# Pinning the sixth form's weight sums of the second MLP's first two pairs in VectorE's program order

## The chip, the cores and the metric

The kernel runs on one core of a Trainium2 chip. Time is device microseconds of one execution, and the median of several executions is what is compared. A profiled execution is slower or faster by a few microseconds than the timed ones, so its own time is given beside it.

## The reference

A two-layer encoder trunk on x of 1024 positions by 1024 features, in float32. Layer 0 mixes tokens by grouped-query attention, layer 1 by a chunked gMLP; each layer ends in a dense squared-ReLU MLP, and every sub-layer is normalized, modulated and added back with a gate:

```
mod = cond @ ada_w[i] + ada_b[i];  sh1, sc1, g1, sh2, sc2, g2 = split(mod, 6)
h = modulate(rmsnorm(x, norm1_g[i]), sh1, sc1)
y = gqa_attention(h, ...) if i % 2 == 0 else chunked_gmlp(h, ...)
x = x + g1 * y
h = modulate(rmsnorm(x, norm2_g[i]), sh2, sc2)
x = x + g2 * (square(relu(h @ w_in[i])) @ w_out[i])      # 1024 -> 4096 -> 1024
```

The change lies in the first product of the second MLP (h @ w_in[1]).

## The kernel before

Everything is kept transposed: features on the 128 partitions, positions along the free axis, in two halves of 512 positions. Every float32 product is made from three faster products: an operand is split into a rounded part "hi" (a cast on ScalarE, L333 for activations, L459 for weights) and a rest "lo" (a subtraction on VectorE, L334 and L460), and TensorE adds hi·hi, hi·lo and lo·hi. The large products further use Winograd's seven-product form of a 2 by 2 block product. Here the blocks of a weight are its quarters: two adjacent 128-column slices of the weight (a "pair") times the two halves of the 1024 inputs. Quarter 11, 12 belong to the pair's first slice (one 512 KB tile `raws[2p]`), 21, 22 to its second (`raws[2p+1]`).

`winograd` runs the first product of each MLP. A unit (q, p) is form q of pair p: twelve 128x512 matmuls (L474 to L476) into one PSUM bank. The second MLP has 16 pairs. With FIRST = 6, forms 1 and 2 of pairs 0 to 5 come first (units 0 to 11), since their activations are ready first; then each pair's forms 6, 5, 4, 7, 3 (pair 0 is units 12 to 16, pair 1 units 17 to 21); pairs 6 and up run all seven forms in a row. The weights of pairs 0 and 1 are loaded whole at the start and stay; those of pairs 2 to 5 pass once for forms 1 and 2 (L427, into t tiles) and are loaded again for the rest. There are four 512 KB buffers of tag w, so pair 2's weights are loaded when pair 0's last readers are done (L421, in `prep` of form 3).

`prep` makes a unit's weights, LA = 3 units ahead of its matmuls in the order of the code. For form 6 it adds quarter 22 to quarter 21 in place (L452) and subtracts quarter 11 from that into quarter 11 (L453). Forms 5, 4, 7 and 3 of the pair all go on from there: form 5 reads the sum in 21; L456 (prepared with form 4) subtracts the new 11 from 12 for form 3; L458 (form 7) subtracts the new 11 from 22. Only form 4's own operand, quarter 22 as loaded, needs none of it. The result goes into one of five s buffers as hi and lo. L482, L485, L488, L490, L493, L496 and L500 are VectorE's readings of the finished products.

What runs between: `mlp` calls a hook after each unit. In the second MLP (HB = 2, 1 and HR = 2, 1, so the second of each) step 1 starts the second half's norm (L280, L282, L287, the power on GpSimd at L242, L294), step 2 calls `forms_b`, steps 3 to 6 make the activations of form 6 (L339, L381, L382, L393 and a split), and steps 7, 8, 9 and 10 split those of forms 5, 4, 7 and 3, four splits each.

The code gives no final order. The framework orders each engine's instructions itself from a model of the machine: an instruction is issued when the model has its inputs ready, an earlier one in the code first where several are ready. Work whose inputs are ready early so floats far ahead of its place in the code. `pin` (L51) takes that freedom away: it puts an instruction behind the one traced just before it on its engine, with no wait. On the chip each engine works its queue in that fixed order and each instruction waits for its own inputs.

The second MLP's first loads and preps are traced two units before the end of the gMLP's output product (`if i == out_.n - PRE: next(mlp1)`); the class `Out` runs that product (matmuls L1215 to L1217, weight casts L1197 and L1198, activations loaded from DRAM by L1173 and split by L333 and L334, PSUM read by L1234 and L1267, weight sums on GpSimd by L1183 and following).

## Time and profile before

| | |
|---|---|
| median of 3 timed executions | 2616.09 us (2610.80 to 2616.37) |
| the profiled execution's own time | 2620.57 us |
| its span, first to last instruction | 2618.8 us |
| TensorE busy | 2593.0 us, 99% of the span |
| VectorE busy | 2179.8 us, 83% |
| ScalarE busy | 1443.7 us, 55% |
| GpSimd busy | 718.5 us, 27% |
| mean granted TensorE clock | 0.998 |
| L452, all 44 instructions | 32.5 us |
| VectorE idle before L452 until a load of the MLPs' first weight landed | 2.4 us, 3 times |

The span lies 1.8 us inside the execution's time; what is outside does not change with an order on VectorE. Busy time of TensorE counts matmuls from start to modelled end and they overlap, so 99% says that it hardly ever stands still, and the idle time before a matmul says where it does. Names such as L452 are lines of the kernel as printed above.

### The profile page before, as it was taken

What the parts mean: (1) busy time and instruction counts of PE and PEld (TensorE: products, weight loads), DVE (VectorE), ACT (ScalarE), POOL (GpSimd) and SP (SyncE); (2) the same over time, 40 slices, a digit from 0 to 9 for tenths busy, and PEclk for the clock granted to TensorE, in tenths of its full rate; (3) what the DMA queues carried; (4) which work ended last, traced back from release to release, by engine and by line L of the source; (5) the groups of instructions that cost most, each with busy time, mean ns of one, the idle gap of its engine ahead of it and who ended that gap; (6) DMA issues with size and microseconds to landing.
All of it is one profiled execution on the core that took longest, in us unless ns stands there. A gap on an engine that the chain in (4) does not pass through costs nothing.

```text
span 2618.8 us, 37177 instructions
## 1 busy us (share of the span) xinstructions
PE 2593.0 (99%) x12808; PEld 2167.8 (83%) x12808; DVE 2179.8 (83%) x3281; ACT 1443.7 (55%) x2584; POOL 718.5 (27%) x527
## 2 busy tenths in 40 slices
PE   9999999999999999999999999999999999999999
PEld 7889999887788888888888888888788788888887
DVE  7878999887989999877987687778889977789974
ACT  4579999845644555345543454445456644455442
POOL 0237876433000005430122055442420000005400
PEclk9999999999999999999999999999999999999999
DMA  8100222233586798544243454568641554497461
GB/s 289 45 1 9 89 82 76 89 130 128 195 284 242 279 310 301 181 137 169 81 153 113 137 175 169 174 216 298 228 142 52 182 176 159 148 313 264 150 212 58
DMA packets 209327, 434.33 MB, mean 166 GB/s; under 512 B 23089, under 2 KB 35505, under 8 KB 209138
## 3 DMA queue, kind: packets, MB, share of 16 engines
q1 hardware_dynamic: 182258, 394.19, 44.7%
q10 hardware_dynamic: 26880, 37.76, 4.0%
q8 instruction: 101, 1.65, 0.3%
q14 instruction: 88, 0.72, 0.1%
HBM read 309.18 MB, written 122.68 MB: 165 GB/s over the span
## 4 chain that ended last, share of the span: by engine, by line
PE 83%; DVE 9%; DMA 3%; ACT 3%; issue 1%; POOL 1%; SPq 0%; DVEq 0%; ACTq 0%; POOLq 0%
PE w L474 10%; PE w L475 10%; PE w L476 10%; PE out L1215 9%; PE out L1216 9%; PE out L1217 9%; PE s L952 4%; PE o L988 4%; PE t L969 4%; PE v L1574 3%; PE v L1573 3%; PE v L1572 3%; PE mix L1679 1%; DVE t L334 1%; DMA t<-hf 1%
## 5 line engine op out<-in xcount | busy, mean ns | idle before, releaser
L1215 PE MATMUL out<-t,s 128*128 128x512 f32 x1232 | 480.1, 390 | 2.5 <-ACT t L333 2.5
L1216 PE MATMUL out<-t,s 128*128 128x512 f32 x1232 | 480.0, 390 | 1.6 <-DVE t L334 1.6
L1217 PE MATMUL out<-t,s 128*128 128x512 f32 x1232 | 479.4, 390 | 0.0
L474 PE MATMUL w<-t,s 128*128 128x512 f32 x1168 | 458.5, 394 | 1.8 <-DVE c L1683 1.2
L475 PE MATMUL w<-t,s 128*128 128x512 f32 x1168 | 455.2, 390 | 1.8 <-DVE t L334 1.8
L476 PE MATMUL w<-t,s 128*128 128x512 f32 x1168 | 454.7, 389 | 0.0
L334 DVE TENSOR_TENSOR t<-t,t 128x512 fp32r<-128x512 f32 x408 | 323.8, 804 | 27.4 <-ACT t L333 20.2
L333 ACT CAST t<-t 128x512 fp32r<-128x512 f32 x408 | 244.8, 617 | 121.1 <-DMA t<-hf 71.3
L1215 PEld LDWEIGHTS out<-t,s 128*128 128x128 f32 x1232 | 231.6, 188 | 51.6 <-ACT t L333 3.7
L1216 PEld LDWEIGHTS out<-t,s 128*128 128x128 f32 x1232 | 231.7, 188 | 50.4 <-DVE t L334 2.9
L1217 PEld LDWEIGHTS out<-t,s 128*128 128x128 f32 x1232 | 231.7, 188 | 48.4
L459 ACT CAST s<-w 128x512 fp32r<-128x512 f32 x292 | 173.5, 616 | 161.8 <-PE w L476 104.7
L474 PEld LDWEIGHTS w<-t,s 128*128 128x128 f32 x1168 | 219.4, 188 | 49.6 <-issue 3.5
L475 PEld LDWEIGHTS w<-t,s 128*128 128x128 f32 x1168 | 219.4, 188 | 48.7 <-DVE t L334 5.2
L460 DVE TENSOR_TENSOR s<-w,s 128x512 fp32r<-128x512 f32 x292 | 221.8, 766 | 43.7 <-ACT s L459 43.0
L1197 ACT CAST s<-t 128x512 fp32r<-128x512 f32 x240 | 148.4, 621 | 197.2 <-PE out L1217 143.8
L476 PEld LDWEIGHTS w<-t,s 128*128 128x128 f32 x1168 | 219.3, 188 | 45.3
L1198 DVE TENSOR_TENSOR s<-t,s 128x512 fp32r<-128x512 f32 x240 | 195.7, 816 | 63.9 <-ACT s L1197 63.1
L1183 POOL TENSOR_TENSOR w<-w,t 128x512 f32<-128x512 f32 x20 | 33.5, 1684 | 765.7 <-DVE t L334 345.8
L955 DVE TENSOR_REDUCE mx<-s 128x1 f32<-128x1024 f32 x128 | 156.2, 1221 | 27.2 <-PE s L952 25.5
L978 DVE TENSOR_TENSOR t<-t,t 128x512 fp32r<-128x512 f32 x256 | 164.2, 682 | 17.3 <-ACT t L972 16.2
L988 PE MATMUL o<-t,t 128*128 128x256 f32 x1024 | 163.5, 292 | 0.0
(259 smaller groups left out, 5060.7 us busy)
## 6 DMA issues: line engine op xcount, KB each, us to landing
t<-hf SPq DMA_DIRECT2D x320, 256.0 KB, 4.0
hf<-c SPq DMA_DIRECT2D x156, 256.0 KB, 3.1
w<-in_wi_dram SPq DMA_DIRECT2D x64, 512.0 KB, 4.3
hf<-c ACTq DMA_DIRECT2D x96, 256.0 KB, 2.3
w<-in_ada_dram SPq DMA_DIRECT2D x36, 512.0 KB, 4.1
x<-in_ada_dram SPq DMA_DIRECT2D x64, 256.0 KB, 5.9
t<-in_wm_dram SPq DMA_DIRECT2D x64, 256.0 KB, 4.9
wf<-w SPq DMA_DIRECT2D x64, 256.0 KB, 2.9
```

The lines of the kernel that those rows point to most:

```text
L333: S.copy(hi, src)
L334: (eng or V).tensor_tensor(lo, src, f32(hi), ALU.subtract)
L459: S.copy(hi, src)
L460: V.tensor_tensor(lo, src, f32(hi), ALU.subtract)
L474: T.matmul(ps, hi[:, a], th, start=kt == 0, stop=False)
L475: T.matmul(ps, hi[:, a], tl, start=False, stop=False)
L476: T.matmul(ps, lo[:, a], th, start=False, stop=kt == 3)
L988: pin(T.matmul(u.po, vt[st][:, u.g * P : (u.g + 1) * P], src[:, s * 256 : (s + 1) * 256], start=st == 0 and part == 0, stop=st == 7 and pa ...
L1198: V.tensor_tensor(lo, src, f32(hi), ALU.subtract)
L1215: T.matmul(ps, hi[:, a], th, start=begin and kt == 0, stop=False, **g)
L1216: T.matmul(ps, hi[:, a], tl, start=False, stop=False, **g)
L1217: T.matmul(ps, lo[:, a], th, start=False, stop=end and kt == 3, **g)
```

## The change

`winograd` gets a flag that only the second MLP sets (layer == 1). With it, the addition of quarter 22 into quarter 21 for form 6 is pinned for pairs 0 and 1. Computation, tiles, loads and engines stay as they are; the framework makes its order anew from the added constraint.

```
-    def winograd(wsrc, npair, f, sink, first=0, hook=None, begin=None):
+    def winograd(wsrc, npair, f, sink, first=0, hook=None, begin=None, stay_=False):
...
                 a11, a21, a22 = (half(p, c) for c in ("11", "21", "22"))
-                V.tensor_tensor(a21, a21, a22, ALU.add)
+                ins = V.tensor_tensor(a21, a21, a22, ALU.add)
+                if stay_ and p < 2:
+                    pin(ins)
                 V.tensor_tensor(a11, a21, a11, ALU.subtract)
...
-        yield from winograd(lambda m: t["wi"][layer, m], 16, f, sink, FIRST, at, lambda: (cut(8), f.update(fs[0])))
+        yield from winograd(lambda m: t["wi"][layer, m], 16, f, sink, FIRST, at, lambda: (cut(8), f.update(fs[0])),
+                            layer == 1)
```

## The prediction, on record before the result

> **What bounds the kernel now.** I read the page first: is any engine but TensorE a bound?

> ```profile
> span 2618.8 us, 37177 instructions
> PE 2593.0 (99%) x12808; PEld 2167.8 (83%) x12808; DVE 2179.8 (83%) x3281; ACT 1443.7 (55%) x2584; POOL 718.5 (27%) x527
> ```

> TensorE stands still for at most 2618.8 - 2593.0 = 25.8 us of the whole kernel, so no order on VectorE can win more, and one that starves TensorE costs in full: nothing behind it is idle enough to give time back. VectorE's 83% is a mean; what counts is whether it is behind at the places that the four moved instructions leave or enter. So next comes the chain of waits around 1857 us, where L452 (the sum) of the second MLP's pairs 0 and 1 runs today, within the gMLP's output product:

> ```profile
> 1850.43 7.25 DMA w<-in_wi_dram
> ...
> 1862.60 0.46 DVE w L452
> ...
> 1867.63 1.77 DVE t L334
> 1869.43 0.63 ACT t L333
> 1870.14 0.76 PE out L1215
> ```

> The chain that sets the end runs from a load of the MLP's weight through L452 into an activation split and then a matmul. VectorE's timeline of the same place shows why:

> ```profile
> 1855.45 0.68 DVE L1198 TENSOR_TENSOR s<-t,s 128x512 fp32r<-128x512 f32 x1
> 1857.70 0.69 DVE L452 TENSOR_TENSOR w<-w 128x512 f32<-128x512 f32 x1 [1.57 <-DMA w<-in_wi_dram]
> 1858.31 0.68 DVE L334 TENSOR_TENSOR t<-t,t 128x512 fp32r<-128x512 f32 x1
> ...
> 1862.52 1.78 DVE L452 TENSOR_TENSOR w<-w 128x512 f32<-128x512 f32 x1
> 1864.22 0.68 DVE L1267 TENSOR_TENSOR t<-out,t 128x512 f32<-128x512 f32 x1
> 1864.83 1.19 DVE L334 TENSOR_TENSOR t<-t,t 128x512 fp32r<-128x512 f32 x1
> 1865.93 1.78 DVE L1198 TENSOR_TENSOR s<-t,s 128x512 fp32r<-128x512 f32 x1
> 1867.63 1.76 DVE L334 TENSOR_TENSOR t<-t,t 128x512 fp32r<-128x512 f32 x1
> ```

> The first sum holds the queue 1.57 us for its load and 1858.31 - 1857.70 = 0.61 us for itself; the second takes 1864.22 - 1862.52 = 1.70 us. Together 3.88 us, and from the first to the split at 1867.63 the queue never rests, so they are queued straight into that split. TensorE's timeline, and the stretches with the granted clock (busy time of PE, PEld, DVE, ACT and POOL with its instructions; then the clock, the DMA share and GB/s):

> ```profile
> 1859.16 0.39 PE L1217 MATMUL out<-t,s 128*128 128x512 f32 x1
> 1859.74 0.47 PE L1215 MATMUL out<-t,s 128*128 128x512 f32 x1 [0.19 <-ACT t L333]
> ...
> 1867.78 0.39 PE L1217 MATMUL out<-t,s 128*128 128x512 f32 x1
> 1870.14 0.76 PE L1215 MATMUL out<-t,s 128*128 128x512 f32 x1 [1.97 <-ACT t L333]
> ...
> 1873.64 0.39 PE L1217 MATMUL out<-t,s 128*128 128x512 f32 x1
> ```

> ```profile
> 1852.00:1868.00 16.00, 15.81 (x70) 12.60 (x68) 14.43 (x20) 8.44 (x15) 5.59 (x4) 1.00 0.99 372
> 1870.00:1872.00 2.00, 1.86 (x5) 1.50 (x6) 2.00 (x4) 0.21 (x2) 0.00 (x0) 0.54 0.00 0
> 2095.00:2270.00 175.00, 175.00 (x773) 144.96 (x773) 133.28 (x209) 85.26 (x144) 0.00 (x0) 1.00 0.47 162
> ```

> The last row gives the pitch of a matmul, 175.00 / 773 = 0.226 us. So the small stop costs 1859.74 - 1859.16 - 0.23 = 0.35 us, the large one 1870.14 - 1867.78 - 0.23 = 2.13 us. Behind the large one the granted clock is 0.54, and the nine matmuls from 1870.14 to 1873.64 take 3.50 us instead of 9 x 0.226 = 2.03: another 1.47 us. All in all 3.95 us hang on this place.

> [...]

> **The change, part by part.** Pinning adds no instruction, wait or DMA: it moves. Each pinned sum takes with it all that goes on from it, and the rows show how far that work runs ahead today:

> ```profile
> 1992.61 0.69 DVE L453 TENSOR_TENSOR w<-w,w 128x512 f32<-128x512 f32 x1
> ...
> 1997.80 0.69 DVE L456 TENSOR_TENSOR w<-w 128x512 f32<-128x512 f32 x1
> ...
> 2002.86 0.68 DVE L460 TENSOR_TENSOR s<-w,s 128x512 fp32r<-128x512 f32 x1
> ...
> 2006.32 0.68 DVE L460 TENSOR_TENSOR s<-w,s 128x512 fp32r<-128x512 f32 x1
> ...
> 2009.16 0.69 DVE L458 TENSOR_TENSOR w<-w,w 128x512 f32<-128x512 f32 x1
> ```

> By the order of the code these are pair 0's L453 and L456, the rests of its forms 6 and 5, and its L458; pair 1's L453 and L456 lie between them.

> *Removed at 1857 (gain).* Which of the 3.88 us reach TensorE? Not all: GpSimd's four adds run right behind, and each VectorE operation with two inputs in SBUF is stretched beside them (1.19 to 1.78 above against 0.68), sum or no sum.

> ```profile
> 1862.41 6.43 POOL L1183 TENSOR_TENSOR c<-c,t 128x512 f32<-128x512 f32 x4 [11.03 <-DMA t<-in_wgo_dram]
> ```

> Without the sums L1267 can start when its unit's product is there, about 1859.74 + 12 x 0.226 + 0.39 = 1862.8 instead of 1864.22; the three stretched operations follow, and the split ends near 1867.9 instead of 1867.63 + 1.76 = 1869.39, 1.5 us earlier. The stop of 2.13 shrinks to about 0.6, the small one goes, the clock stays up; but with TensorE earlier, the later splits can be late by some tenths. 0.35 + 1.5 + 1.47 is 3.3; I take 3.0. Bounds: 3.95 (all of it), and 0.4 if the loads, which use 0.99 of the DMA time here, keep the splits late and only the small stop goes. What is late next in either case is L333 waiting for `t<-hf`.

> *Where the sums go.* Pair 0 is prepared in step 12 - 3 = 9. The last VectorE instruction traced before it is the last split of form 4's activations, in step 8. Pair 1 (unit 17, step 14) comes behind L488 of pair 0's form 5. In today's queue the first place is the last row here:

> ```profile
> 2034.12 0.68 DVE L485 TENSOR_TENSOR c<-w,c 128x512 f32<-128x512 f32 x1
> ...
> 2042.32 0.68 DVE L482 TENSOR_TENSOR c<-w,c 128x512 f32<-128x512 f32 x1
> 2042.92 0.68 DVE L334 TENSOR_TENSOR t<-t,t 128x512 fp32r<-128x512 f32 x1
> ```

> L485 reads pair 0's finished form 6, so unit 12 is computed before 2034 today, and its weights cannot exist before 2042.92 + 0.68 = 2043.6 in that queue after the change. What does TensorE lose? The stretches of the stage, all engines, and (last row) the matmuls with weights from s buffers alone:

> ```profile
> 2011.40:2024.90 13.50, 13.50 (x61) 11.13 (x60) 13.34 (x22) 10.06 (x16) 0.00 (x0) 1.00 0.00 1
> 2024.90:2041.30 16.40, 14.83 (x64) 11.67 (x63) 16.20 (x28) 13.33 (x25) 0.00 (x0) 1.00 0.38 128
> 2041.30:2053.70 12.40, 12.40 (x56) 10.26 (x55) 11.98 (x20) 9.30 (x18) 0.00 (x0) 1.00 0.26 86
> ```

> ```profile
> 2027.65:2041.30 13.65, 4.06 (x15) 1.00 0.45 154
> ```

> From 2027.65 the second forms of pairs 3 to 5 run, whose weights are split late, and 15 matmuls of pair 0 (twelve of form 6, three of form 5) fill the pauses: 15 x 0.226 = 3.4 us that have no such filler after the change. VectorE is full (13.34 of 13.50, 16.20 of 16.40, 11.98 of 12.40): the sums arrive where it has no room. In its favour, the rests of pair 0's forms 7 and 3 and of pair 1's form 6, L485, and pair 2's L452 and L453, which stand ahead of 2042.92 today, move behind too: six operations of 2042.92 - 2042.32 = 0.60 us. Of these 3.6 us ScalarE's casts (13.33 of 16.40 busy) allow perhaps 2.4. So the split ends near 2041.2, L452 near 2041.8, the cast of form 5's weights near 2042.5. The chain of waits tells when the second forms end:

> ```profile
> 2033.74 0.62 ACT s L459
> ...
> 2036.98 0.52 ACT t L333
> 2037.54 0.50 PE w L474
> ```

> The last of them starts at 2037.54 for a cast, and on its path lies a floated cast for pair 1's form 6 (0.62), which the pin sends away: start near 2037.0, end 12 x 0.226 = 2.7 us later, near 2039.7. From there TensorE can run pair 0's form 4, whose weights need no sum and whose activations come from just those splits, until about 2042.5, and find form 5 ready. At 2045.1 it has then done 48 + 12 + 12 = 72 matmuls since 2024.9; today 64 until 2041.3 (its row) and 17 more, 80 without the one that both ends cut. Eight fewer are 1.8 us. Seven sums and two rests, 9 x 0.60 = 5.4 us of work, come into a queue that is full until 2053.7, so a few tenths more are lost. I take 2.0 in all. Bounds: 9.5 us (rival 2), and -1.0 if the floated cast leaves the path and nothing starves.

> *Queues past which work moves.* On SP, pair 2's two loads wait for pair 0's last readers, the rests of forms 7 and 3:

> ```profile
> 2029.46 7.14 SPq L421 DMA_DIRECT2D w<-in_wi_dram  x2
> ```

> They come some 15 to 20 us later, and are needed ten units (27 us) behind form 6 of pair 0: covered. Without that cover each microsecond late would be one lost. Pair 1's pin waits for TensorE to finish form 5; behind it VectorE holds L490 and the next rests, three units ahead of their use. GpSimd issues nothing there.

> *Sum.* -3.0 + 2.0 = -1.0 us on the profiled execution's 2620.57, 2619.6; the median of the runs, 4.5 below that execution, becomes 2615.1. I say 2615.

> **The rivals.**

> 1. *The stop at 1870 goes and nothing starves.* For it: the filling between 2027 and 2041 shows that the framework takes whatever is ready. -3.95 - 1.0 = -5 us: 2611. Against: 15 fillers are gone for certain, and VectorE has no room.

> 2. *The start of the MLP starves (the other side).* If form 4's weights are not prepared ahead and VectorE's queue doesn't move up, L452 begins at 2043.6 and form 5's cast ends 0.6 + 0.6 + 0.1 later, at 2044.9. The second forms end at 2037.54 + 2.7 = 2040.3: TensorE stands 4.6 us, with the lost filling of 3.4 that is 8.0, and a stop longer than 1.97 us brings the slow clock again, 1.5: 9.5 us, less 3.0 is +6.5, 2622.6. With VectorE 2.4 us ahead it is +4: 2620. It decides from 5 us of loss at the start.

> 3. *The stop at 1870 stays, since the loads are what is late.* ScalarE's casts there do wait for `t<-hf`; against it, the very cast before the stop waits for VectorE (the chain's L334). -0.4 + 2.0: 2617.7. If the slow clock doesn't follow from the stop, the gain is 3.0 - 1.5 and the result 2616.6, in the same case. [...]

> 4. *The pin changes nothing*, if the model's order already had the sums there. The rows at 1857 refute it; 2616.

> **How the numbers follow.** Forecast 0.42 (2612.5 to 2617.5), rival 1 0.21, rival 2 0.17, rival 3 with the slow-clock case 0.17, rival 4 0.03. About 5 us (0.2%) is what a measurement of this kernel can tell from no change; the three runs alone spread by 5.6. Faster by more: most of rival 1 and a little of the forecast, 0.19. Slower by more: two thirds of rival 2 and some of 3, 0.14. Within: 0.67. The range 2608.5 to 2622 takes in rival 1's 2611 with the runs' spread, and all but the dear end of rival 2.

> **What would show it.** Right: L452 has no load to wait for and none lies between 1850 and 1990; no stop over 1 us near 1868 and a granted clock of 1.00 there; L452 of pair 0 directly behind a split near 2041; matmuls of form 4 before L485. Wrong: a stop at 1868 that still ends on L334 or on `t<-hf`; a stop of 2 us or more between 2030 and 2046, with a granted clock near 0.5 behind it; stops between 2050 and 2070, which would mean that the 5.4 us of moved work were not absorbed.

## The result, and the profile after

The changed kernel takes 2625.17 us in the median of 6 executions (2618.26 to 2628.46), the kernel before 2615.10 us beside it (2610.80 to 2616.37): a ratio of 1.0042, interval 1.0026 to 1.0057. Timed again later with more executions (below) it is 1.0026, interval 1.0015 to 1.0036. So the change makes the kernel slower by some 7 to 11 us, where 1 us faster was forecast; both medians (the second is 2622.95) lie above the forecast range, which ends at 2622.

The profiled execution took 2618.26 us and was the quickest of its six. Its page:

```profile
span 2616.5 us, 37187 instructions
PE 2588.2 (99%) x12808; PEld 2163.6 (83%) x12808; DVE 2179.6 (83%) x3281; ACT 1447.2 (55%) x2584; POOL 716.1 (27%) x527
...
L476 PE MATMUL w<-t,s 128*128 128x512 f32 x1168 | 459.4, 394 | 5.0 <-ACT s L461 4.4
```

The totals tell nothing: TensorE and VectorE are as busy as before, and this span is even shorter than before's. The one new thing is the end of the last line: 4.4 us in which TensorE waited for L461, the cast of a weight (L459 before; the new lines move every number behind them by two or three: the matmuls are L476 to L478, the rest of a weight L462, the subtraction L455, VectorE's reading of the second form L484).

What moved is seen when each product is taken from its first matmul to the next product's first. The stretches of the gMLP's output product and of the second MLP's first product, in the kernel before (columns: length, then busy time and count of PE, PEld, DVE, ACT and POOL, then granted clock, DMA share, GB/s):

```profile
1766.91:2001.65 234.74, 231.86 (x1017) 190.95 (x1016) 205.26 (x289) 119.83 (x209) 62.21 (x41) 0.99 0.58 200
2001.65:2309.93 308.28, 306.40 (x1354) 252.87 (x1352) 248.68 (x395) 168.47 (x286) 1.43 (x1) 1.00 0.47 161
```

and in the changed kernel:

```profile
1760.93:1991.38 230.45, 229.74 (x1017) 189.95 (x1016) 202.69 (x281) 119.70 (x209) 61.96 (x41) 1.00 0.59 200
1991.38:2307.54 316.16, 308.92 (x1353) 253.49 (x1352) 251.45 (x399) 167.81 (x285) 1.01 (x1) 0.99 0.46 157
```

The first gains 234.74 - 230.45 = 4.29 us, the second loses 316.16 - 308.28 = 7.88 us. The stretches that the change doesn't touch differ by a few us from one execution to the next (in the twelve profiles of this study the part ahead of the first MLP takes 630 to 637 us, and the gMLP's part just ahead of its output product 279 to 284 us), which is why a single span misleads here.

The place that the prediction looked at first, VectorE and TensorE about 1868 us, is quiet. The stretches there, in the changed kernel:

```profile
1852.00:1868.00 16.00, 16.00 (x72) 13.24 (x72) 14.93 (x20) 8.20 (x14) 7.37 (x5) 1.00 0.78 282
1868.00:1872.00 4.00, 4.00 (x20) 3.30 (x19) 4.00 (x5) 0.62 (x1) 2.59 (x2) 1.00 0.41 131
```

No stop, and a granted clock of 1.00. The loss lies in the second MLP. TensorE's timeline there:

```profile
2021.70 0.50 PE L478 MATMUL w<-t,t 128*128 128x512 f32 x1 [1.10 <-DVE t L334]
...
2025.54 0.50 PE L476 MATMUL w<-t,t 128*128 128x512 f32 x1 [1.24 <-ACT t L333]
...
2028.59 0.39 PE L478 MATMUL w<-t,t 128*128 128x512 f32 x1
2033.42 0.50 PE L476 MATMUL w<-t,s 128*128 128x512 f32 x1 [4.44 <-ACT s L461]
```

The last second form ends (2028.59), and the next matmul, form 6 of pair 0, starts 4.83 us later. Behind it the clock falls:

```profile
2028.59:2033.42 4.83, 0.39 (x2) 0.00 (x0) 4.40 (x8) 2.87 (x7) 0.00 (x0) 1.00 0.26 98
2033.42:2037.30 3.88, 3.56 (x8) 2.45 (x9) 3.88 (x7) 3.59 (x7) 0.00 (x0) 0.56 0.00 0
```

At the pitch of 0.226 us, the stop costs 4.83 - 0.23 = 4.60, the eight matmuls behind it 3.88 - 1.81 = 2.07 (0.32 of them a second wait, for the rest of the weight), the two smaller stops 1.26 and 1.40 (1.10 and 1.24 of idleness, and 0.16 each by which a matmul's modelled duration of 0.39 is longer than the pitch). Together 9.3; before had one stop here, 1.57 us of idleness, 1.73 in all. 9.3 - 1.7 = 7.6 of the 7.88; the rest are stops of tenths.

Why form 6 comes so late is on VectorE's timeline and, in the last row, ScalarE's:

```profile
2029.02 0.69 DVE L484 TENSOR_TENSOR c<-w,c 128x512 f32<-128x512 f32 x1 [1.25 <-PE w L478]
2029.63 1.28 DVE L334 TENSOR_TENSOR t<-t,t 128x512 fp32r<-128x512 f32 x2
2030.83 0.68 DVE L452 TENSOR_TENSOR w<-w 128x512 f32<-128x512 f32 x1
2031.43 0.68 DVE L334 TENSOR_TENSOR t<-t,t 128x512 fp32r<-128x512 f32 x1
2032.03 0.68 DVE L455 TENSOR_TENSOR w<-w,w 128x512 f32<-128x512 f32 x1
```

```profile
2032.75 0.62 ACT L461 CAST s<-w 128x512 fp32r<-128x512 f32 x1 [0.83 <-DVE w L455]
```

At the head of VectorE's queue stands L484, the reading of the very second form that TensorE is just computing: it waits 1.25 us for it, and the sum stands three operations behind. So form 6 cannot begin before the second form has ended and six operations of VectorE and a cast have followed. And nothing else is there for TensorE. The casts of weights into s buffers, in the changed kernel between 1975 and 2037 us and in the one before between 1985 and 2046 (duration min/median/max in ns, then first and last start):

```profile
L461 ACT CAST s<-w x7: 603/618/626, 1981.0 to 2034.8; 128x512 fp32r<-128x512 f32 x7
```

```profile
L459 ACT CAST s<-w x11: 605/622/627, 1991.2 to 2045.6; 128x512 fp32r<-128x512 f32 x11
```

The seven are four ahead of the MLP (1981 to 1989, forms 1 and 2 of pairs 0 and 1) and three from 2032.75 on (forms 6, 5 and 4 of pair 0, by the order of the code). Before, form 6, 5 and 4 of pair 0 followed the first four at 2001.85, 2005.58 and 2007.78. Form 4, which needs no sum, came behind form 6 all the same.

### The profile page after: what moved, and what is told of

It is laid out like the page before. It is cut to its first block, busy times and chain, and to the rows that moved or that the text cites. A ratio compares the mean times of both kernels' runs of the same rounds, so it can differ in the third digit from the quotient of the medians.

```text
span 2616.5 us, 37187 instructions
## 1 busy us (share of the span) xinstructions
PE 2588.2 (99%) x12808; PEld 2163.6 (83%) x12808; DVE 2179.6 (83%) x3281; ACT 1447.2 (55%) x2584; POOL 716.1 (27%) x527
## 4 chain that ended last, share of the span: by engine, by line
PE 87%; DVE 7%; ACT 2%; DMA 2%; issue 1%; SPq 0%; POOL 0%; DVEq 0%; ACTq 0%
PE out L1218 11%; PE out L1217 11%; PE out L1219 11%; PE w L476 10%; PE w L478 10%; PE w L477 10%; PE s L954 4%; PE o L990 4%; PE t L971 4%; PE v L1577 3%; PE v L1576 3%; PE v L1575 3%; PE mix L1682 2%; DVE t L334 1%; PE wo L926 1%
## 5 line engine op out<-in xcount | busy, mean ns | idle before, releaser
L1217 PE MATMUL out<-t,s 128*128 128x512 f32 x1232 | 479.2, 389 | 1.1 <-ACT t L333 1.1
L476 PE MATMUL w<-t,s 128*128 128x512 f32 x1168 | 459.4, 394 | 5.0 <-ACT s L461 4.4
L478 PE MATMUL w<-t,s 128*128 128x512 f32 x1168 | 455.3, 390 | 0.3 <-DVE s L462 0.3
L334 DVE TENSOR_TENSOR t<-t,t 128x512 fp32r<-128x512 f32 x408 | 326.2, 810 | 26.2 <-ACT t L333 18.9
L333 ACT CAST t<-t 128x512 fp32r<-128x512 f32 x408 | 245.0, 617 | 114.0 <-DMA t<-hf 63.3
L461 ACT CAST s<-w 128x512 fp32r<-128x512 f32 x292 | 174.4, 617 | 182.6 <-PE w L478 125.4
L1217 PEld LDWEIGHTS out<-t,s 128*128 128x128 f32 x1232 | 231.2, 188 | 49.6 <-ACT t L333 1.5
L1218 PEld LDWEIGHTS out<-t,s 128*128 128x128 f32 x1232 | 231.3, 188 | 49.5 <-DVE t L334 1.9
L1219 PEld LDWEIGHTS out<-t,s 128*128 128x128 f32 x1232 | 231.3, 188 | 48.0
L476 PEld LDWEIGHTS w<-t,s 128*128 128x128 f32 x1168 | 219.7, 188 | 52.7 <-ACT s L461 5.0
L478 PEld LDWEIGHTS w<-t,s 128*128 128x128 f32 x1168 | 219.6, 188 | 46.2 <-DVE s L462 0.9
L462 DVE TENSOR_TENSOR s<-w,s 128x512 fp32r<-128x512 f32 x292 | 220.1, 760 | 41.6 <-ACT s L461 41.1
```

The costliest lines, as they stand in the source:

```text
L333: S.copy(hi, src)
L334: (eng or V).tensor_tensor(lo, src, f32(hi), ALU.subtract)
L461: S.copy(hi, src)
L462: V.tensor_tensor(lo, src, f32(hi), ALU.subtract)
L476: T.matmul(ps, hi[:, a], th, start=kt == 0, stop=False)
L478: T.matmul(ps, lo[:, a], th, start=False, stop=kt == 3)
```

## The experiments

For each kernel the ratio to the kernel before on the same chip, and the two stretches read from its profile as above (before: 234.7 and 308.3 us):

| kernel | ratio, interval | gMLP output product | second MLP's first product |
|---|---|---|---|
| before, again | one execution | 231.8 | 308.3 |
| the change | 1.0042, 1.0026 to 1.0057 | 230.5 | 316.2 |
| the change, again | 1.0026, 1.0015 to 1.0036 | 231.3 | 316.3 |
| sums free, subtraction pinned | 1.0032, 1.0021 to 1.0044 | 233.4 | 316.1 |
| only pair 0 pinned | 1.0025, 1.0014 to 1.0036 | 232.6 | 316.4 |
| only pair 1 pinned | 0.9989, 0.9980 to 0.9997 | 230.5 | 308.3 |
| change, form 4 ahead | 1.0013, 1.0004 to 1.0021 | 230.5 | 313.9 |
| both pinned, step 7 | 1.0011, 1.0001 to 1.0020 | 230.7 | 312.6 |
| both pinned, step 4 | 1.0009, 0.9999 to 1.0020 | 230.8 | 313.2 |
| both pinned, start of the MLP | 1.0002, 0.9993 to 1.0011 | 230.5 | 309.5 |
| both pinned, behind the second unit's weights | 0.9985, 0.9976 to 0.9993 | 230.5 | 308.2 |

**The kernel before, once more.** No edit; it asks how much of the gain is the execution's.

> The kernel before once more, unchanged, for a second profile of it. In the first profile the gMLP's output product lasted 234.75 us and held the stop of 2.13 us with the slow clock at 1868, the second MLP's first product 308.27 us. Theory A (the change wins 4 us at 1868 and loses 8 us at the start of the second MLP): the stop is there again, 233 to 235 us, and 308 us behind it. Theory C (the stop at 1868 was that one execution's, so that the change has nothing to win there): no stop over 1 us at 1868 and about 230.5 us, as after the change.

Measured: the MLP's product is the same to 0.01 us, the gMLP's output product 2.95 us shorter than in the first profile. The stop near 1868 was only 0.76 us of idleness here, without a slow clock, and 231.8 lies between the two theories' figures. So 2.95 of the 4.29 us that the first profile offered to gain there are not there every time.

**The sums free, the subtraction pinned.** Both sums are traced at step 6 without a pin, so that they run in the gMLP as before; L453's subtraction is pinned in their place.

```
-                V.tensor_tensor(a21, a21, a22, ALU.add)
-                V.tensor_tensor(a11, a21, a11, ALU.subtract)
+                if not (stay_ and p < 2):
+                    V.tensor_tensor(a21, a21, a22, ALU.add)
+                ins = V.tensor_tensor(a11, a21, a11, ALU.subtract)
+                if stay_ and p < 2:
+                    pin(ins)
...
+            if stay_ and i == 6:
+                for p in range(2):
+                    V.tensor_tensor(half(p, "21"), half(p, "21"), half(p, "22"), ALU.add)
```

> The loss without the gain: the sums of pairs 0 and 1 float into the gMLP as before the change, but the subtraction behind each (quarter 11 from the sum) is pinned where the change pins the sum. Theory A (late weights of pair 0's form 6 and nothing to fill TensorE's wait): the second MLP's first product takes 315 to 317 us as after the change, against 308.3 before; time 6 to 9 us above the kernel before. Rival B (the two sums' own time on a full VectorE): two of the seven moved operations are not moved, so 2 us less than after the change, about 314. Rival C (the loss is one execution's): 308.

Measured: 316.1 us, the changed kernel's loss in full (its stop is shorter and the slow clock behind it longer), with VectorE doing no sum of these pairs in the MLP. What costs is that form 6 of pair 0 comes late, whichever of its two operations is held back. The stop before form 6, and a stop in the gMLP that came back with the sums, on TensorE's timeline:

```profile
1868.96 0.47 PE L1221 MATMUL out<-t,s 128*128 128x512 f32 x1 [1.95 <-ACT t L333]
...
2040.00 0.79 PE L477 MATMUL w<-t,s 128*128 128x512 f32 x1 [3.24 <-ACT s L462]
```

**Both sums pinned at the start of the MLP**, ahead of the loop over the units (here and wherever they are traced in another place below, `prep` leaves them out):

```
+        if stay_:
+            for p in range(2):
+                pin(V.tensor_tensor(half(p, "21"), half(p, "21"), half(p, "22"), ALU.add))
         for i in range(len(units)):
```

> The gain without the loss: both sums are traced and pinned at the start of the second MLP's first product, ahead of its first unit's step, so they leave the gMLP but come before all that goes on from them, which floats as before. Theory A: the gMLP's output product takes 230.5 us without a stop at 1868, the MLP's first product 308 to 309; time equal to the kernel before where its executions don't have the stop, up to 4 us below where they do. Rival B (the sums' time on a full VectorE at the MLP's start costs): first product 310 or more and the time 2 us or more above the kernel before.

Measured: the gMLP keeps the gain, and the MLP loses only 309.5 - 308.3 = 1.2 us, between theory A's 309 and the rival's 310; the two sums run 2.3 us into the MLP, and three stops of 0.46, 0.62 and 1.16 us are left. The ratio can't be told from 1.

**The change with form 4 of pair 0 ahead.** In step 8 form 4's weight is cast and split, ahead of the pinned sum, and its matmuls are traced ahead of form 6's:

```
+            if stay_ and i == 8:
+                w_ = wide("s", F32R)
+                sf[("4", 0)] = w_[:, :512], w_[:, 512:]
+                S.copy(w_[:, :512], half(0, "22"))
+                V.tensor_tensor(w_[:, 512:], half(0, "22"), f32(w_[:, :512]), ALU.subtract)
...
+            if stay_ and i == 12:
+                ahead[("4", 0)] = product("4", 0)
```

> The kernel after the change, with pair 0's form 4 (whose weights need no sum) prepared in step 8 ahead of the pinned sum, and its twelve matmuls ahead of form 6's. Theory A (TensorE has nothing to fill the wait for form 6 because form 4's s buffer and matmuls stand behind form 6 in the order): the stop of 4.83 us at 2029 shrinks to 1 to 2.5 us and the slow clock behind it goes, first product 311 to 313 us instead of 316.2, time 3 to 5 us below the changed kernel. Rival B (VectorE is the limit, whatever TensorE does meanwhile): the stop only moves, 315 to 316 us.

Measured: 313.9 us, 2.3 less than the change, 0.9 above theory A's range and below the rival's. This is the filling that the prediction had counted on: it takes its twelve matmuls out of the stop, and no more. ScalarE's timeline, TensorE's, and a stretch:

```profile
1995.02 0.63 ACT L528 CAST s<-w 128x512 fp32r<-128x512 f32 x1 [1.30 <-PE out L1236]
```

```profile
2034.84 0.39 PE L484 MATMUL w<-t,s 128*128 128x512 f32 x1
2036.87 0.50 PE L482 MATMUL w<-t,s 128*128 128x512 f32 x1 [1.64 <-ACT s L465]
2037.21 0.40 PE L483 MATMUL w<-t,s 128*128 128x512 f32 x1
2038.03 0.50 PE L484 MATMUL w<-t,s 128*128 128x512 f32 x1 [0.42 <-DVE s L466]
```

```profile
2038.87:2040.87 2.00, 2.00 (x6) 1.54 (x5) 2.00 (x4) 1.01 (x3) 0.00 (x0) 0.50 0.00 0
```

The cast of form 4 now runs at 1995.02, 41 us ahead of form 6's (2036.20); its twelve matmuls end at 2034.84, and the stop behind them is 1.64 us of idleness instead of 4.44: 2.8 less, which is 12 x 0.226 = 2.7. But the clock falls here too (0.50), and the two stops of 1.10 and 1.26 us ahead of it remain: 5.6 us of the loss are still there.

**The change once more**, in one comparison with the next three:

> The changed kernel once more, beside the three variants and in the same rounds. Theory A (by the stretches of the profiles so far: the output product of the gMLP 2.9 us shorter, the first product of the second MLP 7.9 us longer): about +5 us, ratio 1.0015 to 1.0025. Rival: the first comparison's +11 us (1.0042) is all of the change, and something outside these two stages is longer too: then over +8 us, and a stretch other than these two differs by more than it differs between two profiles of the kernel before (2.4 us at the start, 0.6 in the others).

Measured: the two stretches come to 231.3 and 316.3, the ratio 1.0026 is +6.8 us on 2617.1. That lies between the two theories' figures; the first comparison's +11 isn't borne out by any other stretch, and the intervals of the two overlap.

**Both pinned behind the second unit's weights.** The sums are traced in the loop that prepares the first three units, behind the second one:

```
         for i in range(LA):
             prep(i)
+            if stay_ and i == 1:
+                for p in range(2):
+                    pin(V.tensor_tensor(half(p, "21"), half(p, "21"), half(p, "22"), ALU.add))
```

> Both sums stay in the second MLP, but are traced and pinned behind the preparation of its second unit's weights, some 35 us ahead of where the change puts pair 0's. Theory A (the loss is pair 0's sixth form coming late): first product of the second MLP 308.3 to 309.5 us as before, output product of the gMLP 230.5 as in the changed kernel (234.8 and 231.8 in two profiles of before), so -1.5 to -3 us against before, ratio 0.9988 to 0.9995. Rival (VectorE has no room for the moved work in the second MLP, wherever it stands): the first product stays 3 us or more longer than 308.3, and the ratio is 1.0000 or above.

Measured: faster than before, and so than the change: 0.9985, interval 0.9976 to 0.9993, in the median 2612.65 against 2617.08 us. Of these 4.4 us the two stretches explain 1.3 to 4.3 (the gMLP's product took 231.8 and 234.7 us before). Its stretches and the sums on VectorE:

```profile
1762.64:1993.13 230.49, 229.78 (x1017) 189.94 (x1016) 204.28 (x285) 119.51 (x209) 62.88 (x41) 1.00 0.59 201
1993.13:2301.34 308.21, 306.38 (x1354) 252.81 (x1352) 249.65 (x397) 168.51 (x286) 1.38 (x1) 1.00 0.47 161
```

```profile
1986.44 0.68 DVE L512 TENSOR_TENSOR w<-w 128x512 f32<-128x512 f32 x1
1987.04 0.68 DVE L264 TENSOR_TENSOR t<-t,t 128x512 f32<-128x512 f32 x1
1987.64 0.68 DVE L512 TENSOR_TENSOR w<-w 128x512 f32<-128x512 f32 x1
```

The sums are still within the gMLP's output product, some 6 us ahead of the MLP, but some 130 us later than before: no load to wait for, and no split of that product was late for them. It keeps the gain and has none of the loss. It doesn't refute the rival: the moved work is not in the MLP.

**Only pair 0, and only pair 1 pinned.** The condition of the pin is `p == 0` in the one, `p == 1` in the other.

> Only pair 0's sum is pinned where the change has it; pair 1's floats into the gMLP as before. Theory A: the whole loss is pair 0's, so the first product of the second MLP takes 315 to 316.5 us as in the changed kernel, and the gMLP's output product between 230.5 and 233: +4 to +8 us against before, ratio 1.0015 to 1.003. Rival (both pairs share the loss, since VectorE is full there): 311 to 313 us, ratio near 1.001.

> Only pair 1's sum is pinned; pair 0's floats into the gMLP as before and waits there for its load. Theory A: first product of the second MLP 308 to 309 us, the gMLP's output product 230.5 to 234.5, ratio 0.999 to 1.0005. Rival (both pairs share the loss): 311 to 313 us, ratio near 1.001.

Measured: 316.4 us with pair 0 alone, 308.3 with pair 1 alone. The whole loss is pair 0's; pair 1's sum costs nothing in the MLP, though VectorE is full around it (6.00 us of the 6.00 from 2036 to 2042). That is against the rival. For the gain it is the other way round, as far as one profile each can tell: pair 0's sum does no harm in the gMLP, as its stretch is 230.5, while with pair 1's left there a stop stays. Each waits for its load. VectorE's rows of the kernel with pair 0 floating, of the one with pair 1 floating, and the latter's stop on TensorE:

```profile
1854.02 0.69 DVE L452 TENSOR_TENSOR w<-w 128x512 f32<-128x512 f32 x1 [1.70 <-DMA w<-in_wi_dram]
```

```profile
1863.75 0.69 DVE L452 TENSOR_TENSOR w<-w 128x512 f32<-128x512 f32 x1 [2.46 <-DMA w<-in_wi_dram]
```

```profile
1870.40 0.47 PE L1217 MATMUL out<-t,s 128*128 128x512 f32 x1 [1.55 <-ACT t L333]
```

In these two profiles only the sum at 1863, right ahead of three operations that run slowly (1.29 to 1.78 us each here; 1.19 to 1.78 in the prediction's rows, beside GpSimd), reaches TensorE; that its place is the reason is likely, but not tested.

**Both pinned at step 4, and at step 7.** In the loop over the units, `if stay_ and i == 4` (or 7) ahead of `prep`. This asks from where on the place in the order costs.

> Both sums pinned at the start of step 4 of the second MLP, five steps ahead of where the change puts pair 0's. Theory A (what costs is that form 6 of pair 0 is not ready when the second forms of pairs 3 to 5 need filling and then end): form 6 has its weights some 13 us earlier than in the changed kernel, so no stop of 4.4 us and no slow clock behind it, some filling back: first product of the second MLP 308.5 to 311 us, ratio 0.9985 to 1.000. Rival (two sums of 0.6 us each ahead of the splits of this stage, where VectorE is full, cost by themselves): 311 us or more.

> Both sums pinned at the start of step 7, two steps ahead of where the change puts pair 0's: behind the four splits of form 6's activations. Theory A: form 6's cast comes some 6 us earlier than in the changed kernel, about when the second forms end, so the stop of 4.4 us shrinks to under 1 us and the slow clock goes, while the two stops of 1.1 and 1.2 us ahead of it stay for want of filling: first product 310 to 312.5 us, ratio 0.9995 to 1.001. Rival (the order of the s buffers keeps form 6 late whenever the sums stand behind the first forms): 315 us or more.

Measured: 313.2 and 312.6 us; both miss theory A's ranges, the first by 2, the second by a tenth. At step 7 the large stop did become small (0.32 us before form 6), but stops of 1.70 and 1.30 us stand elsewhere, and behind the first the clock fell. At step 4 form 6's weight was cast at 2017.75, before the second forms needed filling, and yet there is a stop of 3.23 us. ScalarE's timeline and TensorE's of that kernel:

```profile
2035.74 1.14 ACT L460 CAST s<-w 128x512 fp32r<-128x512 f32 x2 [1.34 <-DVE w L459]
2036.79 0.61 ACT L333 CAST t<-t 128x512 fp32r<-128x512 f32 x1
2037.31 0.62 ACT L1355 ACTIVATE c<-c 128x512 f32<-128x512 f32 x1
2037.84 0.60 ACT L333 CAST t<-t 128x512 fp32r<-128x512 f32 x1
...
2038.49 0.50 PE L475 MATMUL w<-t,t 128*128 128x512 f32 x1 [3.23 <-ACT t L333]
```

and the subtraction on VectorE:

```profile
2034.98 0.68 DVE L459 TENSOR_TENSOR w<-w,w 128x512 f32<-128x512 f32 x1
```

Here the casts of pair 0's next weights stand at the head of ScalarE's queue and wait 1.34 us for a subtraction on VectorE, and the cast that TensorE needs for a second form stands behind them. The rival's "311 us or more" has the number. Its reason is neither shown nor refuted: VectorE is busy without a break from 2014 to 2037 (23.00 us of 23.00), so the subtraction stands in a full queue, but the two sums take 1.2 us and the loss is 4.9. It is not form 6's lateness. So the lateness of form 6 is the cause of the changed kernel's stop, but not a rule for every place. What holds over these places, one profile each: with the sums 6 us ahead of the MLP nothing is lost, 2.3 us into it 1.2 us, 15 us into it 4.9, 29 us into it 4.3, and 39 us into it (the change: 2030.83 - 1991.38) 7.9.

## Why the prediction was wrong, step by step

**The bound, and the gain of 3.0.** Right in place, and near in size on the mean, which is in part luck. TensorE's stops decide, the one at 1868 is gone, and no L452 is left between 1850 and 1990. The profile on which the sum was made gave 4.29, a little over the bound of 3.95; the bound itself is short by one matmul, since eight matmuls, not nine, lie between the start at 1870.14 and that at 1873.64, so that the slow clock cost 3.50 - 1.81 = 1.69 and all in all 4.17 hung on the place. The three profiles with both sums in the gMLP (234.7, 231.8, 233.4) have a mean of 233.3, the seven with none there (230.45 twice, 230.46, 230.49, 230.65, 230.81 and 231.27) 230.65: 2.7 us. What was misread is the share of the pieces. By the one profile each of the two kernels with one sum left there, it is the second sum that reaches the split; and the slow clock, half of the 3.0, came in one of the three profiles only: with the sums free and the subtraction pinned a stop of 1.95 us of idleness at the same place brought none (its rows stand below).

**Where the sums go.** Right. The MLP starts 2001.65 - 1991.38 = 10.27 us earlier in this execution, so the sum, from 2030.83 to 2031.51, stands at 2041.1 to 2041.8 on before's clock (the prediction: directly behind a split that ends near 2041.2, done near 2041.8), and the last second form ends at 2028.59 + 0.39 + 10.27 = 2039.25 (near 2039.7). VectorE's queue did move up, by 2.5 us (2.4 were allowed for).

**"From there TensorE can run pair 0's form 4, whose weights need no sum".** This is the step that failed. Its weights do need no sum, but they were not there: no cast of form 4 ran between 1989 and 2032.75, and its own came third, behind forms 6 and 5. Form 4 stands in the code behind forms 6 and 5, which wait for the sum. That its place there is the reason, and not some other input, is shown by the kernel in which it is prepared ahead of the sum: its cast floats to 1995.02, and the stop shrinks by just its twelve matmuls. With the subtraction pinned it is the same for form 5, whose operand is the sum and is there from 1858 on: no weight is cast into an s buffer between 1996.63 and 2039.33, and then form 6's comes first. That the place counts by way of the five s buffers, which would be taken in the order of the code, is the likely reading and not tested by itself: that kernel moved the asking for the buffer, the cast and the matmuls together, and none has more buffers. The prediction looked at a unit's data and not at its turn.

The second half of the same step failed too: "until about 2042.5, and find form 5 ready". Form 6 went first, and its weight needs a further split and the subtraction behind the sum, 1.2 us of VectorE. Its cast ended at 2033.37, 2043.6 on before's clock, and its first matmul came at 2043.7. Where the prediction counted 72 matmuls from 2024.9 to 2045.1 against 80 before, the changed kernel's trace has 50 in that stretch (2014.63 to 2034.83 on its own clock).

**The loss of 2.0.** Mis-sized by this step: 7.9 measured, 5.9 more, within its bounds of -1.0 and 9.5. The missing form 4 is 2.3 of the 5.9 (the kernel with form 4 ahead). The rest came at the same stop: form 6's longer way, and a slow clock that the 2.0 did not hold and that only rival 2 had named. How the rest divides between these was not tested. The lost filling was named right: the stops of 1.10 and 1.24 us stay with form 4 ahead.

**"Seven sums and two rests ... a few tenths more are lost."** The four more VectorE instructions in the MLP's stretch (399 against 395) were absorbed: with pair 1 alone pinned the stretch is as before, and the changed kernel has no stop over 0.3 us between 2038 and 2080; stops there would have been the prediction's sign that they were not.

**The queues past which work moves.** Covered, as said: pair 2's loads go out at 2040.57, 2050.8 on before's clock, 21 us later than the 2029.46 of the prediction's row, and the sum of pair 2 at 2048.51 waits for none. That of pair 3 does wait for its load, at no cost to TensorE:

```profile
2040.57 1.58 SPq L421 DMA_DIRECT2D w<-in_wi_dram  x2
```

```profile
2061.48 0.69 DVE L452 TENSOR_TENSOR w<-w 128x512 f32<-128x512 f32 x1 [1.39 <-DMA w<-in_wi_dram]
```

**The rivals.** What happened is rival 2, in its milder case: form 4 not prepared ahead, VectorE ahead in time. The prediction's own sign of being wrong came with it: a stop of over 2 us between 2030 and 2046, and a clock near 0.5 behind it. Its dear case, with VectorE not ahead, had a stop of 4.6 us, lost filling of 3.4 and a slow clock of 1.5; in the milder one the stop is 2.4 shorter. Measured were 4.60, and 2.07 behind it. That the 4.60 is the dear case's figure is luck: VectorE was 2.5 us ahead, but form 6's way was longer than form 5's, which the rival had counted with. It gave 2620 with VectorE 2.4 us ahead and 2622.6 without; the medians are 2625.17 and 2622.95. Its chance of 0.17 was too small: it hung on one question that the code answers, which unit stands ahead of which, and not on chance. Rival 1 (nothing starves) is what the sums pinned behind the second unit's weights give, 4.4 us faster; it needs another place. Rivals 3 and 4 fell: the stop at 1868 is gone. Of rival 3's second case, that the slow clock doesn't follow from the stop, so much is true that it followed in one of three profiles.

**The slow clock behind the stop.** The prediction let the 1.47 us of slow clock go with the stop, from one row, in which the clock fell to 0.54 behind 1.97 us of idleness. With more rows: the clock fell behind 4.44 us of idleness (0.56 in the changed kernel's row above), but also behind 3.24 (0.50, with the subtraction pinned) and 3.23 (at step 4, where the matmuls behind it soon follow at 0.43 us instead of 0.226), behind the 1.97 of the first profile, behind 1.70 with the sums at step 7 (0.50), and behind 1.64 followed by 0.42 with form 4 ahead (0.50); behind 1.95 (1.00, with the subtraction pinned), 1.57 (1.00, before's stop in the MLP) and 1.55 (only pair 0 pinned, the matmuls behind it at 0.23 us) it did not. So the length of a stop does not decide by itself. Cut where the granted clock changes (the first two rows of the second fence: at a whole multiple of 3.413 us ahead of its change), the first profile, the one with the subtraction pinned (three rows) and the one with the sums at step 7 read:

```profile
1866.74:1870.15 3.41, 1.44 (x8) 0.89 (x6) 3.41 (x4) 1.76 (x3) 2.11 (x2) 1.00 0.48 142
1870.15:1873.56 3.41, 3.41 (x8) 2.73 (x9) 3.41 (x7) 1.67 (x3) 0.00 (x0) 0.50 0.28 99
1873.56:1876.98 3.42, 3.42 (x16) 2.82 (x16) 3.42 (x7) 0.62 (x1) 0.83 (x1) 1.00 0.66 208
```

```profile
1865.32:1868.73 3.41, 1.69 (x8) 1.07 (x6) 3.41 (x3) 1.63 (x3) 2.34 (x2) 1.00 0.47 144
1868.73:1872.15 3.42, 3.17 (x13) 2.39 (x14) 3.42 (x7) 1.63 (x4) 0.00 (x0) 1.00 0.33 81
2039.40:2046.22 6.82, 6.22 (x14) 4.51 (x15) 6.79 (x12) 5.62 (x11) 0.00 (x0) 0.50 0.10 38
```

```profile
2023.26:2026.67 3.41, 1.71 (x7) 1.07 (x7) 3.41 (x7) 1.38 (x4) 0.00 (x0) 1.00 0.00 0
2026.67:2030.09 3.42, 3.42 (x10) 2.52 (x9) 3.42 (x7) 3.39 (x7) 0.00 (x0) 0.50 0.21 77
```

In the kernel before's profile the clock was 0.50 from 477.51 to 480.92 us too, and from there to the fall at 1870.15 it is 1389.23 us, 407 times 3.4133; in the changed kernel's it was 0.50 from 2033.90 to 2037.31. In the 3.41 us just ahead of a fall TensorE stood still for 2.93 us (3.41 - 0.48) in the changed kernel, for 1.97 (3.41 - 1.44) in the first profile, for 1.70 (3.41 - 1.71) with the sums at step 7, and ahead of 477.51 for 0.10 (3.41 - 3.31); with the subtraction pinned it stood still for 1.72 (3.41 - 1.69) and the clock stayed at 1.00. The stop of 1.95 us lay across two such stretches, 1.72 and 0.23 us of it. What decides whether the clock falls is not shown.

## What to carry to other kernels

When work is moved behind other work in a kernel whose order a framework makes, ask of everything that is to cover the gap not only whether its data are ready but whether its turn has come: here a unit that needed nothing stood behind one that waited, most likely for the next buffer of a shared ring. An operation that floats too early was better pinned just ahead of the stage that needs it (2612.65 us) than in the step that uses it (2622.95). Compare stage by stage and over several profiles: untouched stages differed here by 5 to 6 us, as much as the change is worth.

## What the runs showed of the hardware that was not expected

The same program stops differently from one execution to the next. In the kernel before, TensorE was idle at the same place for 1.97 us in one profile and for 0.76 in the other, and the gMLP's output product took 234.7 and 231.8 us, while the MLP's product agreed to 0.01 us. The DMA share is higher in the former (0.58 against 0.47); whether that is the reason isn't shown.
